# Two blocks of a language model on one core: rounded x at one address relation to the weights, with new segments and a smaller descriptor ring

## The chip, the cores and the metric

One core of one Trainium2 chip runs the whole program. The metric is the device time of one execution in microseconds; of repeated runs the median counts.

## The reference

Two transformer blocks in sequence on 512 tokens of width 1024, all in float32. The first norms x, projects it by `w_in`, and joins three branches (gated linear attention, a gated short convolution, attention in a window of 128) by sigmoid gates; the second puts 16 meta tokens ahead (528 rows), projects by `w_in_2`, and has an HGRN2 branch of 8 heads beside a Mamba-2 branch. Each ends in an FFN with a depthwise convolution of 3 taps. Cut to what is touched:

```python
def first_block(x, ...):
    u = rmsnorm(h, g_mix[l])
    z = u @ w_in[l]
    ...
    h = h + merged @ w_o[l]
    u = rmsnorm(h, g_ffn[l])
    hid = causal_dwconv(u @ w_up[l], ffn_conv_w[l])
    h = h + (jax.nn.silu(hid[..., :D_FF]) * hid[..., D_FF:]) @ w_down[l]
    return rmsnorm(h, g_final)

def second_block(x, meta_tokens, ...):
    h = jnp.concatenate([meta, x], axis=1)
    u = rmsnorm_2(h, norm1_w[l])
    proj = u @ w_in[l]
    ...
    h = h + jnp.concatenate([out_a, out_b], axis=-1) @ w_out[l]
    h = h + conv_glu_ffn(rmsnorm_2(h, norm2_w[l]), ...)
    return rmsnorm_2(h, final_norm_w)[:, N_META:, :]
```

## The kernel before, in words

Everything is feature-major: channels on the 128 partitions, tokens along the free dimension. The residual stream is `H`, 8 row groups (k) of 528 floats. A float32 product is made of three matmuls on rounded operands (float32r): `split` (L190) makes the high part on ACT and the remainder on DVE, for x into `XH` and `XL`; `WStream` does the same for the weights, `wh` and `wl`. The rms factor is not in x: it is multiplied in when a product is evacuated, so projections start before the norm's sums are done.

`WStream` (L53) loads all weights in the order in which the program takes them, in chunks of 8 tiles of 128 x 128 (1024 floats a partition, a load of 512 KB from SP's queue). `prep_to` casts a chunk to `wh` on ACT (L83) and subtracts for `wl` on DVE (L84); `take` asks for that two chunks ahead. `wraw` has two buffers, `wh` and `wl` three each, allocated in one row after the constants.

`gemm` (L234) runs over k and calls `pass3` (L228): for each k the matmuls of `wh` with `XH`, `wh` with `XL`, `wl` with `XH`, each over every segment, with the weights as the stationary operand and x as the moving one. A segment is a stretch of columns that fits a PSUM bank: block 1 has one of 512, block 2 two. After each k `tick` lets the lanes, generators with the work of the heads and scans, put a few small instructions in between; this and the order of the calls set the order on every queue, and the tile framework adds the waits. At the end of a product its evacuation runs on DVE and ACT.

Where x is used: block 1's `w_in` product with 512 columns (L528; the values product, L565, has x as the stationary operand), the gates, and the first FFN's up projection (`ffn`, L686); block 2's `w_in_2` product with `segs` of 264 + 264 for what needs the meta tokens and `segq` of 256 + 258 for what needs only the last 514 columns; the second FFN's up projection with 256 + 258. `FH`/`FL` hold the hidden layer of an FFN for its down projection, `MH`/`ML` the merged branches, `BH`/`BL` the branch outputs, `YH`/`YL` block 2's mixer output. Several pools start with a tile of 512 bytes (`pad1`, `pad2`, `pad3`) between a high part and its remainder.

The lines that place x:

```python
self.H = c.tile([P, KD, L], F32, name="H")
self.XH = c.tile([P, KD, L], F32R, name="XH")
self.XL = c.tile([P, KD, L], F32R, name="XL")
self.par_t = c.tile([P, NPAR], F32, name="par_t")
cm = c.tile([P, 3 * P + 24], F32, name="cm")
```

L is 528 and P is 128; `par_t` and `cm` take 2048 and 1632 bytes of a partition, `wraw` two times 4096, and then the `wh` buffers follow. Block 1 uses columns 8 to 520 of a row (`X1 = 8`), block 2 all 528.

Block 2's Mamba-2 branch loads tables from DRAM by POOL's queue (`m2_core`, L851: `seg` and `ei` for each chunk of 128 tokens); POOL's descriptors lie in a ring in SBUF ahead of the first tile, 16 KB of each partition by default.

Of the kernel before, what the change touches and what calls it, by code (L numbers as in the profile page):

```python
# [9 lines left out]
F32 = mybir.dt.float32  # L10
F32R = mybir.dt.float32r
# [7 lines left out]
P = 128  # L19
D = 1024  # L20
T = 512
META = 16
L = T + META
PADL = T + 32
X1 = 8
KD = D // P
NFF = 22
EPS = 1e-6
# [99 lines left out]
class Builder:  # L128
# [177 lines left out]
    def setup(self):  # L306
        nc, c = self.nc, self.const
        self.H = c.tile([P, KD, L], F32, name="H")
        self.XH = c.tile([P, KD, L], F32R, name="XH")
        self.XL = c.tile([P, KD, L], F32R, name="XL")  # L310
        self.par_t = c.tile([P, NPAR], F32, name="par_t")
        cm = c.tile([P, 3 * P + 24], F32, name="cm")
        self.four = cm[:, 3 * P:3 * P + 16]
        self.ident, self.le, self.ones = (cm[:, i * P:(i + 1) * P] for i in range(3))
        nc.scalar.preload_act_table_set("exp_and_others")
        nc.sync.dma_start(out=self.H[:, 0, META:L], in_=self.ins["xT"][:, 0])
        nc.scalar.dma_start(out=self.par_t[:, 0:8], in_=self.ins["par"][:, 0:8])
        self.W.load_to(0)
        for k in range(1, KD):
            nc.sync.dma_start(out=self.H[:, k, META:L], in_=self.ins["xT"][:, k])  # L320
            if k == 2:
                self.W.load_to(1)
        nc.gpsimd.dma_start(out=self.par_t[:, 8:NPAR], in_=self.ins["par"][:, 8:NPAR])
        nc.gpsimd.dma_start(out=cm[:, 0:3 * P + 16], in_=self.ins["cm"])
        nc.gpsimd.dma_start(out=self.H[:, :, 0:META], in_=self.ins["metaT"])

    def X(self, c0=META):
        return lambda k: (self.XH[:, k, :], self.XL[:, k, :])

    def sumsq(self, acc, k, src):  # L330
        if k == 0:
# [169 lines left out]

    def block1(self):
        nc, tc = self.nc, self.tc
        H, XH, XL = self.H, self.XH, self.XL
        self.W.prep_to(0)
        sums = [self.sq_acc(), self.sq_acc()]

# [9 lines left out]
            self.act(t, h, AF.Square)  # L517
            eng.tensor_tensor(out=sums[k % 2], in0=sums[k % 2], in1=t, op=ALU.add)
        for k in range(KD):
            self.split(XH[:, k, X1:X1 + T], XL[:, k, X1:X1 + T], H[:, k, META:L], self.par("g_mix", k))  # L520
            if k > 2:
                square(k - 3)
        for k in range(KD - 3, KD):
# [1 line left out]
        Rt = self.stat.tile([P, 4], F32, tag="Rt", name="Rt", bufs=1)  # L525
        R = self.r_tile()
        Rx = R[:, META:L]
        segs = [(X1, T)]  # L528
        X = self.X()
        WI = lambda c: [("w_in", k, c) for k in range(KD)]  # L530

        with ExitStack() as s1:
# [10 lines left out]
            with ExitStack() as s2:  # L543
# [14 lines left out]
                with tc.tile_pool(reuse_waits="tile", name="sp", bufs=1) as sp:  # L558
                    self.dist = sp.tile([P, 256], F32, name="dist")
                    nc.gpsimd.dma_start(out=self.dist, in_=self.ins["dist"])  # L560
                    sk = sp.tile([P, T], F32, name="sk")
                    svt = sp.tile([P, 4, P], F32, name="svt")
                    sq = [sp.tile([P, T], F32, name=f"sq{t}") for t in range(4)]
                    accs = [self.acc() for _ in range(4)]
                    for k in range(KD):  # L565
                        wh, wl = self.W.take([("w_in", k, GV + m * P) for m in range(4)])
                        for b in range(4):
                            c = slice(X1 + b * P, X1 + (b + 1) * P)
                            for i, (x, w) in enumerate(((XH, wh), (XL, wh), (XH, wl))):
                                self.mm(accs[b], x[:, k, c], w, start=k == 0 and i == 0, stop=k == 7 and i == 2)  # L570
                        if k == 5:
                            self.norm(self.token_rstd(sums, D, R, META, Rt), 4)
                        self.tick(4)

                    def ev_gv(a):
                        for b in range(4):
                            self.act(self.GVt[:, b, :], a[b], AF.Copy, scale=Rt[:, b:b + 1])
                    self.pend.append((ev_gv, accs))
                    self.flush(2)
                    self.lanes[1].add(self.meta_norm(), 6)  # L580
                    self.gemm16(wga, self.par("g_mix", 0, KD), [(META, T)], 3,
                                lambda a: self.mul(self.GAt[0:96], a[0][0:96], Rx[0:96]))
                    self.gemm(WI(SK), X, segs, lambda a: self.mul(sk, a[0], Rx))
                    sv = sp.tile([P, T], F32, tag="pT", name="sv", bufs=2)

                    def sv_gen():
                        ps = self.sm()
                        for n in range(4):
                            self.tr(ps[:, n * P:(n + 1) * P], sv[:, n * P:(n + 1) * P])
                        nc.scalar.copy(svt.rearrange("p a b -> p (a b)"), ps)  # L590
                        yield 1
                    self.gemm(WI(SV), X, segs, lambda a: self.mul(sv, a[0], Rx))
                    self.lanes[0].add(sv_gen(), 3)
                    for t in range(4):
                        self.gemm(WI(("sq", t)), X, segs,
                                  lambda a, t=t: self.stt(sq[t], a[0], 0.125, Rx, ALU.mult, ALU.mult))
                    self.flush(0, 1)
                    self.lanes[0].add(self.swa(sp, sq, sk, svt), 3)
                    sgr = [br.tile([P, T], F32, tag=f"blg{i}", name=f"sgr{i}") for i in range(4)]
                    for h in range(4):  # L600
                        def ev_gr(a):
                            t = gp.tile([P, T], F32, tag="a1", name="gr", bufs=1)
                            self.mul(sgr[h], a[0], Rx)
                            self.act(t, sgr[h], AF.Sigmoid)
                            self.mul(sgr[h], sgr[h], t)
                        self.gemm(WI(GR + h * P), X, segs, ev_gr)
                    glas = []
                    for h in range(4):
                        q = gp.tile([P, T], F32, tag="q", name="q", bufs=2)
                        kk = gp.tile([P, T], F32, tag="kk", name="kk", bufs=2)  # L610
                        self.gemm(WI(GQ + h * P), X, segs,
                                  lambda a: self.stt(q, a[0], float(P) ** -0.5, Rx, ALU.mult, ALU.mult))
                        self.gemm(WI(GK + h * P), X, segs, lambda a: self.mul(kk, a[0], Rx))
                        self.lanes[2].add(self.gla_head(gp, h, q, kk, sgr[h]), 2)
                    self.flush(0, 1)
# [48 lines left out]
            for m in range(KD):  # L664
                def ev_o(a, m=m):
                    h = H[:, m, META:L]
                    self.add(h, h, a[0])
                    self.split(XH[:, m, X1:X1 + T], XL[:, m, X1:X1 + T], h, self.par("g_ffn", m))
                    self.sumsq(sqa, m, h)
                self.gemm([("w_o", k, m * P) for k in range(KD)], lambda k: (MH[:, k, :], ML[:, k, :]), [(0, T)], ev_o)  # L670
        R = self.r_tile()
# [3 lines left out]
        nc.gpsimd.tensor_tensor(out=g1, in0=self.par("g_final", 0, 8), in1=self.par("norm1", 0, 8), op=ALU.mult)  # L675

        def after(m, h, _):
            self.split(XH[:, m, META:L], XL[:, m, META:L], h, g1[:, m:m + 1])
            self.split(XH[:, m, 0:META], XL[:, m, 0:META], H[:, m, 0:META], self.par("norm1", m))
            self.sumsq(sqh, m, h)  # L680
            self.ts(h, h, self.par("g_final", m), ALU.mult)
            self.sumsq(sqg, m, h)
# [3 lines left out]
    def ffn(self, up, cw, cb, down, R, after, zero):  # L686
        nc, tc, H = self.nc, self.tc, self.H
        W = T + 2
        segs = [(X1, T)] if zero else [(META - 2, 256), (META + 254, 258)]
        rsegs = [(META, T)] if zero else segs  # L690
        Xb = (self.XH, self.XL)
        with tc.tile_pool(reuse_waits="tile", name="fp", bufs=1) as fp:
            FH = fp.tile([P, NFF, T], F32R, name="FH")
            fp.tile([P, P], F32, name="pad3")
# [1 line left out]
            for j in range(NFF):  # L696
                cs = []
                for i in range(2):
# [6 lines left out]
                    def ev(a, i=i, f=f, u=u, c=c, cs=cs, j=j):  # L705
# [13 lines left out]
                        else:  # L719
                            self.mul(c, cs[0], c)  # L720
                            self.split(FH[:, j, :], FL[:, j, :], c)
                    self.gemm([(up, k, f * P) for k in range(KD)],
                              lambda k: (Xb[0][:, k, :], Xb[1][:, k, :]), segs, ev)
                    cs.append(c)
            for m in range(KD):
                def ev_d(a):
# [338 lines left out]

    def block2(self, sqh, sqg):
        nc, tc, st = self.nc, self.tc, self.stat
        H, XH, XL = self.H, self.XH, self.XL
        W2 = T + 2
        R = self.r_tile()  # L1070

# [20 lines left out]
                self.mul(H[:, k, META:L], H[:, k, META:L], R1[:, META:L])  # L1092
                yield 6
        self.norm(norm2(), 10)
        segs = [(0, 264), (264, 264)]
        segq = [(META - 2, 256), (META + 254, 258)]
        X = self.X()
        WI = lambda c: [("w_in_2", k, c) for k in range(KD)]

        with ExitStack() as sy:  # L1100
# [173 lines left out]
            with tc.tile_pool(reuse_waits="tile", name="hp", bufs=1) as hp:  # L1274
# [55 lines left out]
                def ev_o(m):  # L1330
                    def ev(a):
                        h = H[:, m, META - 2:L]
                        for ps, (c0, n) in zip(a, [(0, 256), (256, 258)]):
                            self.add(h[:, c0:c0 + n], h[:, c0:c0 + n], ps[:, 0:n])
                        self.split(XH[:, m, META - 2:L], XL[:, m, META - 2:L], h, self.par("norm2", m))
                        self.sumsq_w(sqa, m, h, W2)
                    return ev
                def y_k(i):
# [168 lines left out]
```

## Time and profile before

| | |
|---|---|
| median of 3 runs | 1769.63 us (1768.66 to 1769.98) |
| the profiled execution | 1771.67 us, of which span 1769.8 us |
| granted clock of TensorE, mean | 0.997 |
| busy: PE, PEld, DVE, ACT, POOL | 1738.0, 1534.6, 1089.8, 729.7, 123.9 us |
| read from HBM, written | 156.93 MB, 2.18 MB |

PE is TensorE's matmuls, PEld its loads of stationary operands, which run beside matmuls. A matmul is shown from its start to the modelled end of its pipeline, so consecutive ones overlap, and the spacing of starts is what a stream of them costs. The profile's clock is a share of 2.4 GHz. Block 1 runs to about 868 us: the values product and the branches to about 250, gates and branch products to about 455, `w_o` to about 500, the FFN's up projection to about 745 and its down projection to 868. Block 2 has the mixer to 1285, the output projection to 1365, the up projection to 1631 and the down projection after it.

### The profile page before, as it was taken

To read this page: it belongs to the slowest core of one execution; us is meant where nothing else is said; L and a number is where in the kernel's file an instruction comes from. 1 tells how busy PE (TensorE), PEld (TensorE's weight loads), DVE (VectorE), ACT (ScalarE), POOL (GpSimd) and SP (SyncE) were. 2 spreads that over 40 slices of the span, in tenths; PEclk is the share of its full clock that TensorE was granted. 3 is DMA by queue.
4 is the path that set the end of the run, shared out by engine and by line. 5 is a ranking of instruction groups with operands and counts; after the bars stand their busy time and mean duration, and the time that the engine had idled before them with its cause. 6 is when DMAs were issued, how large, how long until landed. Compare 5 with 4: busy or idle time off the path is not lost. (4 is left out here: it accounts for less than half of the span.)

```text
span 1769.8 us, 26970 instructions
## 1 busy us (share of the span) xinstructions
PE 1738.0 (98%) x11014; PEld 1534.6 (87%) x11014; DVE 1089.8 (62%) x1923; ACT 729.7 (41%) x1175; POOL 123.9 (7%) x203
## 2 busy tenths in 40 slices
PE   8999999999999999999998999999999999999997
PEld 6777778888888888888897999999999999999885
DVE  4476774444457777734488789767643667766332
ACT  4355443222344444433356545545432444444221
POOL 2000000000110000001112221000001000000000
PEclk9999999999999999999999999999999999999999
DMA  5222223332333333233333322122223223332331
GB/s 184 84 72 60 64 80 96 96 96 95 96 95 94 93 94 95 92 100 101 88 101 126 113 86 72 61 73 72 72 84 96 84 96 95 86 95 96 96 89 67
DMA packets 45691, 160.84 MB, mean 91 GB/s; under 512 B 5472, under 2 KB 5616, under 8 KB 45568
## 3 DMA queue, kind: packets, MB, share of 16 engines
q1 hardware_dynamic: 42480, 149.83, 27.3%
q0 software_dynamic: 2800, 9.03, 1.6%
q8 instruction: 86, 1.41, 0.3%
q14 instruction: 37, 0.30, 0.1%
q10 hardware_dynamic: 288, 0.27, 0.0%
HBM read 156.93 MB, written 2.18 MB: 90 GB/s over the span
## 5 line engine op out<-in xcount | busy, mean ns | idle before, releaser
L181 PE MATMUL acc<-XH,wh 128*128 128x512 f32 (+3 forms) x2320 | 633.2, 326 | 0.1
L181 PE MATMUL acc<-XL,wh 128*128 128x512 f32 (+3 forms) x2320 | 621.1, 321 | 0.0
L181 PE MATMUL acc<-XH,wl 128*128 128x512 f32 (+3 forms) x2320 | 619.0, 320 | 0.0
L83 ACT CAST wh<-wraw 128x1024 fp32r<-128x1024 f32 (+1 forms) x279 | 292.0, 1047 | 507.8 <-PE acc L181 441.8
L84 DVE TENSOR_TENSOR wl<-wraw,wh 128x1024 fp32r<-128x1024 f32 (+1 forms) x279 | 342.6, 1228 | 218.8 <-ACT wh L83 211.4
L181 PEld LDWEIGHTS acc<-XH,wh 128*128 128x128 f32 x2320 | 385.1, 189 | 45.2 <-issue 9.8
L181 PEld LDWEIGHTS acc<-XH,wl 128*128 128x128 f32 x2320 | 385.3, 189 | 33.8 <-issue 0.5
L181 PEld LDWEIGHTS acc<-XL,wh 128*128 128x128 f32 x2320 | 385.9, 189 | 32.9 <-issue 0.5
L181 PE MATMUL acc<-FH,wh 128*128 128x512 f32 x352 | 137.8, 392 | 0.0
L181 PE MATMUL acc<-FH,wl 128*128 128x512 f32 x352 | 137.1, 390 | 0.0
L181 PE MATMUL acc<-FL,wh 128*128 128x512 f32 x352 | 137.0, 389 | 0.0
L164 DVE SCALAR_TENSOR_TENSOR c<-u,par_t,c 128x512 f32<-128x512 f32 x176 | 131.8, 749 | 6.7 <-ACT c L178 3.7
L152 DVE TENSOR_TENSOR u<-acc,R 128x512 f32<-128x512 f32 (+2 forms) x132 | 63.8, 510 | 87.9 <-PE acc L181 84.7
L336 POOL TENSOR_TENSOR sqa<-sqa,sqt 128x512 f32<-128x512 f32 x27 | 40.8, 1513 | 735.5 <-ACT sqt L178 735.5
L181 PEld LDWEIGHTS acc<-FH,wl 128*128 128x128 f32 x352 | 66.1, 188 | 14.0
L181 PEld LDWEIGHTS acc<-FL,wh 128*128 128x128 f32 x352 | 66.1, 188 | 13.5
L181 PEld LDWEIGHTS acc<-FH,wh 128*128 128x128 f32 x352 | 66.1, 188 | 13.4
L178 ACT ACTIVATE FH<-c 128x512 fp32r<-128x512 f32 x44 | 27.8, 632 | 116.0 <-DVE c L152 116.0
L178 ACT ACTIVATE c<-u,par_t 128x512 f32<-128x512 f32 x88 | 67.6, 768 | 2.4 <-DVE u L152 2.2
L152 DVE TENSOR_TENSOR H<-H,acc 128x512 f32<-128x512 f32 (+2 forms) x41 | 22.6, 569 | 74.6 <-PE acc L181 74.6
L178 ACT ACTIVATE c<-c 128x512 f32<-128x512 f32 x44 | 27.8, 632 | 83.5 <-DVE c L164 83.5
L181 PE MATMUL acc<-yh,wh 128*128 128x256 f32 (+1 forms) x256 | 51.4, 282 | 0.1
(393 smaller groups left out, 1967.1 us busy)
## 6 DMA issues: line engine op xcount, KB each, us to landing
wraw<-in_wts SPq DMA_DIRECT2D x277, 512.0 KB, 3.6
seg<-cumd POOLq DMA_DIRECT2D x10, 512.0 KB, 4.3
H<-in_xT SPq DMA_DIRECT2D x8, 256.0 KB, 9.6
ei<-eid POOLq DMA_DIRECT2D x16, 128.0 KB, 3.3
out<-H SPq DMA_DIRECT2D x7, 256.0 KB, 2.7
wraw<-in_wts SPq DMA_DIRECT2D x2, 256.0 KB, 4.6
r<-in_r POOLq DMA_DIRECT2D x1, 272.0 KB, 3.2
r<-in_r POOLq DMA_DIRECT2D x1, 256.0 KB, 8.3
```

The costliest lines, as they stand in the source:

```text
L83: self.nc.scalar.copy(h[:, e], t[:, e])
L84: self.nc.vector.tensor_tensor(out=l[:, e], in0=t[:, e], in1=h[:, e].bitcast(F32), op=ALU.subtract)
L152: self.nc.vector.tensor_tensor(out=out, in0=a, in1=b, op=op)
L164: self.nc.vector.scalar_tensor_tensor(out=out, in0=a, scalar=s, in1=b, op0=op0, op1=op1)
L178: self.nc.scalar.activation(out=out, in_=a, func=func, scale=scale, **kw)
L181: self.nc.tensor.matmul(out, lhsT, rhs, start=start, stop=stop)
L336: self.nc.gpsimd.tensor_tensor(out=acc, in0=acc, in1=t, op=ALU.add)
```

## The change

The tiles of rounded x become flat: 8 x 640 floats each, with 512 bytes (`padx`) between the two, and two views of them. `X1` is block 1's and the first FFN's, rows of 512 floats one behind the other; `X2` is block 2's and the second FFN's, 528 columns of rows of 640 floats. Both begin 24 floats (96 bytes) into the tile. Segments are counted from the view's first column; in block 2 264 + 264 becomes 256 + 272, and the second FFN's x is written from column 0 of the row instead of 14. The three edits together take 7680 bytes more of each partition, and the ring of POOL's descriptors is cut from 16 KB to 8 KB.

```diff
@@ -22,7 +22,8 @@
...
 PADL = T + 32
-X1 = 8
+X0 = 24
+XW = 640
 KD = D // P
...
@@ -306,8 +307,13 @@
...
         self.H = c.tile([P, KD, L], F32, name="H")
-        self.XH = c.tile([P, KD, L], F32R, name="XH")
-        self.XL = c.tile([P, KD, L], F32R, name="XL")
+        self.X1, self.X2 = [], []
+        for n in ("XH", "XL"):
+            x = c.tile([P, KD * XW], F32R, name=n)
+            self.X1.append(x[:, X0:X0 + KD * T].rearrange("p (k t) -> p k t", t=T))
+            self.X2.append(x.rearrange("p (k t) -> p k t", t=XW)[:, :, X0:X0 + L])
+            if n == "XH":
+                c.tile([P, P], F32, name="padx")
         self.par_t = c.tile([P, NPAR], F32, name="par_t")
...
@@ -324,8 +330,8 @@
...
 
-    def X(self, c0=META):
-        return lambda k: (self.XH[:, k, :], self.XL[:, k, :])
+    def X(self, x):
+        return lambda k: (x[0][:, k, :], x[1][:, k, :])
 
...
@@ -501,7 +507,7 @@
...
         nc, tc = self.nc, self.tc
-        H, XH, XL = self.H, self.XH, self.XL
+        H, (XH, XL), (XH2, XL2) = self.H, self.X1, self.X2
         self.W.prep_to(0)
...
@@ -517,7 +523,7 @@
...
         for k in range(KD):
-            self.split(XH[:, k, X1:X1 + T], XL[:, k, X1:X1 + T], H[:, k, META:L], self.par("g_mix", k))
+            self.split(XH[:, k, :], XL[:, k, :], H[:, k, META:L], self.par("g_mix", k))
             if k > 2:
...
@@ -525,8 +531,8 @@
...
         Rx = R[:, META:L]
-        segs = [(X1, T)]
-        X = self.X()
+        segs = [(0, T)]
+        X = self.X(self.X1)
         WI = lambda c: [("w_in", k, c) for k in range(KD)]
...
@@ -565,7 +571,7 @@
...
                         for b in range(4):
-                            c = slice(X1 + b * P, X1 + (b + 1) * P)
+                            c = slice(b * P, (b + 1) * P)
                             for i, (x, w) in enumerate(((XH, wh), (XL, wh), (XH, wl))):
...
@@ -665,7 +671,7 @@
...
                     self.add(h, h, a[0])
-                    self.split(XH[:, m, X1:X1 + T], XL[:, m, X1:X1 + T], h, self.par("g_ffn", m))
+                    self.split(XH[:, m, :], XL[:, m, :], h, self.par("g_ffn", m))
                     self.sumsq(sqa, m, h)
...
@@ -675,8 +681,8 @@
...
         def after(m, h, _):
-            self.split(XH[:, m, META:L], XL[:, m, META:L], h, g1[:, m:m + 1])
-            self.split(XH[:, m, 0:META], XL[:, m, 0:META], H[:, m, 0:META], self.par("norm1", m))
+            self.split(XH2[:, m, META:L], XL2[:, m, META:L], h, g1[:, m:m + 1])
+            self.split(XH2[:, m, 0:META], XL2[:, m, 0:META], H[:, m, 0:META], self.par("norm1", m))
             self.sumsq(sqh, m, h)
...
@@ -686,9 +692,9 @@
...
         W = T + 2
-        segs = [(X1, T)] if zero else [(META - 2, 256), (META + 254, 258)]
-        rsegs = [(META, T)] if zero else segs
-        Xb = (self.XH, self.XL)
+        segs = [(0, T)] if zero else [(0, 256), (256, 258)]
+        rsegs = [(META, T)] if zero else [(META - 2, 256), (META + 254, 258)]
+        X = self.X(self.X1 if zero else self.X2)
         with tc.tile_pool(reuse_waits="tile", name="fp", bufs=1) as fp:
...
@@ -720,7 +726,7 @@
...
                     self.gemm([(up, k, f * P) for k in range(KD)],
-                              lambda k: (Xb[0][:, k, :], Xb[1][:, k, :]), segs, ev)
+                              X, segs, ev)
                     cs.append(c)
...
@@ -1065,7 +1071,7 @@
...
         nc, tc, st = self.nc, self.tc, self.stat
-        H, XH, XL = self.H, self.XH, self.XL
+        H, (XH, XL) = self.H, self.X2
         W2 = T + 2
...
@@ -1092,9 +1098,9 @@
...
         self.norm(norm2(), 10)
-        segs = [(0, 264), (264, 264)]
+        segs = [(0, 256), (256, 272)]
         segq = [(META - 2, 256), (META + 254, 258)]
-        X = self.X()
+        X = self.X(self.X2)
         WI = lambda c: [("w_in_2", k, c) for k in range(KD)]
...
@@ -1332,7 +1338,7 @@
...
                             self.add(h[:, c0:c0 + n], h[:, c0:c0 + n], ps[:, 0:n])
-                        self.split(XH[:, m, META - 2:L], XL[:, m, META - 2:L], h, self.par("norm2", m))
+                        self.split(XH[:, m, 0:W2], XL[:, m, 0:W2], h, self.par("norm2", m))
                         self.sumsq_w(sqa, m, h, W2)
...
@@ -1495,7 +1501,7 @@
...
 
-    nc = _bacc.Bacc("TRN2", target_bir_lowering=False, num_devices=1)
+    nc = _bacc.Bacc("TRN2", target_bir_lowering=False, num_devices=1, dynamic_dma_scratch_size=8192)
     ins = {n: nc.dram_tensor(f"in_{n}", s, F32, kind="ExternalInput").ap() for n, s in IN_SHAPES.items()}
...
```

## Rows read from the trace of the kernel before

**Rows 1.** The page: busy time by engine, granted clock in 40 slices.

```profile
PE 1738.0 (98%) x11014; PEld 1534.6 (87%) x11014; DVE 1089.8 (62%) x1923; ACT 729.7 (41%) x1175; POOL 123.9 (7%) x203
...
PEclk9999999999999999999999999999999999999999
```

**Rows 2.** Waits of PE, the two longest (us in total, times, longest).

```profile
PE sm L184 <- DVE xf L164: 6.4, 3, 2.8
PE acc L181 <- ACT XH L178: 5.8, 1, 5.8
```

**Rows 3.** Groups of matmuls by shape, 512 columns (count, busy us, mean ns).

```profile
L181 PE MATMUL acc<-XH,wh 128*128 128x512 f32 x784 | 312.5, 399 | 0.0
...
L181 PE MATMUL acc<-XH,wl 128*128 128x512 f32 x784 | 309.3, 394 | 0.0
...
L181 PE MATMUL acc<-FH,wh 128*128 128x512 f32 x352 | 137.8, 392 | 0.0
...
L181 PE MATMUL acc<-MH,wh 128*128 128x512 f32 x64 | 24.9, 389 | 0.0
...
L181 PE MATMUL acc<-bh_gla,wh 128*128 128x512 f32 x32 | 12.6, 394 | 0.0
...
L181 PE MATMUL acc<-bh_conv,wh 128*128 128x512 f32 x32 | 12.4, 389 | 0.0
```

**Rows 4.** PE by window: length, busy (matmuls), clock, DMA share, GB/s.

```profile
520.00:720.00 200.00, 200.00 (x865) 1.00 0.32 98
760.00:860.00 100.00, 100.00 (x442) 1.00 0.30 95
1390.00:1610.00 220.00, 220.00 (x1844) 1.00 0.29 92
1310.00:1360.00 50.00, 50.00 (x422) 1.00 0.33 96
```

**Rows 5.** Timeline of PE, 303 to 313 us (start, duration, instruction).

```profile
304.72 0.39 PE L181 MATMUL acc<-bh_conv,wh 128*128 128x512 f32 x1
...
308.80 0.39 PE L181 MATMUL acc<-XH,wh 128*128 128x512 f32 x1
...
309.50 0.39 PE L181 MATMUL acc<-XH,wh 128*128 128x512 f32 x1
...
310.19 0.40 PE L181 MATMUL acc<-XH,wh 128*128 128x512 f32 x1
...
311.59 0.39 PE L181 MATMUL acc<-XH,wh 128*128 128x512 f32 x1
```

**Rows 6.** Preparation of a weight chunk on ACT and DVE, and its load.

```profile
L83 ACT CAST wh<-wraw 128x1024 fp32r<-128x1024 f32 x277 | 290.8, 1050 | 505.9 <-PE acc L181 441.8 <-issue 59.6 <-DMA wraw<-in_wts 2.8
...
L84 DVE TENSOR_TENSOR wl<-wraw,wh 128x1024 fp32r<-128x1024 f32 x277 | 341.2, 1232 | 212.0 <-ACT wh L83 204.6 <-PE sm L181 4.3
...
wraw<-in_wts SPq DMA_DIRECT2D x277, 512.0 KB, 3.6
```

**Rows 7.** Both FFNs' up projections by window: PE, PEld, DVE, ACT, POOL.

```profile
500.00:745.00 245.00, 245.00 (x1068) 198.82 (x1067) 173.53 (x228) 106.07 (x136) 6.44 (x46) 1.00 0.30 95
...
1365.00:1631.00 266.00, 266.00 (x2228) 265.81 (x2227) 182.33 (x289) 110.47 (x140) 3.69 (x2) 1.00 0.29 92
```

**Rows 8.** Groups by shape in block 2: a matmul of 264 columns, evacuations.

```profile
L181 PE MATMUL acc<-XH,wh 128*128 128x264 f32 x448 | 96.1, 295 | 0.1
...
L152 DVE TENSOR_TENSOR u<-acc,R 128x256 f32<-128x256 f32 x44 | 18.7, 425 | 43.5 <-PE acc L181 43.5
...
L152 DVE TENSOR_TENSOR mu<-acc,R 128x264 f32<-128x264 f32 x24 | 9.4, 425 | 1.7 <-PE acc L181 1.6
```

**Rows 9.** POOL's burst (timeline), `seg` loads, ACT's wait for them.

```profile
921.62 1.12 POOL L864 DMA_DIRECT2D seg<-cumd  x2 [0.61 <-DMA cumd<-ct]
...
seg<-cumd POOLq DMA_DIRECT2D x10, 512.0 KB, 4.3
...
L178 ACT ACTIVATE seg<-seg,dv 128x128 f32<-128x128 f32 x64 | 20.5, 390 | 16.8 <-DMA seg<-cumd 14.5 <-PE acc L181 2.1
```

## The prediction

> **What bounds the kernel now.** I read the page from the top. TensorE is busy for 98% of the span at a granted clock of 1.00 (the 2.4 GHz level) from the first slice to nearly the last, and DVE, the next engine, for 62% [rows 1]. The list of PE's waits is short: the largest two, 6.4 us for `xf` in block 2 and 5.8 us for `XH` at the start, are most of it [rows 2]. The chain that ended last covers 3% of the span and says nothing on the middle. So the kernel is as long as its stream of matmuls, and the question is how far apart their starts are.
>
> Next the groups of matmuls by shape, because a change of addresses can only show where equal shapes take different times. They do: a matmul of 512 columns has a mean of 389 ns when its moving operand is `MH` or `bh_conv`, 392 for `FH`, and 394 to 399 for `XH` and `XL` [rows 3]. A duration holds the pipeline's depth, so the spacing of starts is read from counts. In the up projection of the first FFN (moving `XH`, `XL`) 865 matmuls lie in 200 us, 231.2 to 231.8 ns each, depending on how the two at the edges count; in its down projection (moving `FH`, `FL`) 442 lie in 100 us, 226.2 to 227.3 ns [rows 4]. One stage shows both back to back: the `conv` and `swa` products from 304.72 to 308.80 us are 18 steps, 226.7 ns each, and the gate product that follows takes 12 steps to 311.59 us, 232.5 ns each [rows 5]. Same shape, engines and clock, so the operands' place is the suspect.
>
> The tile sizes give that place. A weight tile of a chunk is 512 bytes wide, so all weights start at one remainder modulo 512. `FH`, `FL`, `MH`, `ML` and the `bh`/`bl` tiles have rows of 2048 bytes and, with the pads, start at that remainder: relation 0 on every k. Rows of `XH` are 2112 bytes, so the relation moves by 64 from k to k and is 0 only once in eight, at k = 1. After the change it comes to 0 for every k of block 1: from row 0 of `XH` to the first weight tile there are 20480 + 512 + 20480 + 2048 + 1632 + 8192 - 96 = 53248 bytes, 104 times 512. Net, memory moves by 7680 - 8192 = -512 bytes, so every later pool keeps its relation.
>
> **The change, part by part.**
>
> *Block 1, moving x.* 784 k-steps of three matmuls (`wh` with `XH`, `wh` with `XL`, `wl` with `XH`), 2352 in all [rows 3]. I take 226.7 ns, the pace of `conv`/`swa`, in place of 231.7. In the gates (192 steps) and the first FFN's up projection (352) nothing interrupts the stream: 1632 x 5.0 ns = 8.2 us. The other 240 steps run before 250 us, with the small matmuls of gla and attention between them. After a break the pace doesn't come back at once: the gla products, also at relation 0 but just behind a gate product at another one, have a mean of 394 ns, and `conv` behind them has 389 [rows 3]. I take 4 of the 5 ns: 720 x 4 = 2.9 us. The gla products gain the same entry: 96 x about 4 ns = 0.4 us. Sum -11.5 us; bounds -12.2 (all at 5 ns) and -4.2 (rival 2).
>
> *Cover for a faster stream.* A chunk of weights feeds 24 matmuls: 5.56 us before, 5.44 after. It needs 1.05 us of ACT, 1.23 us of DVE and 3.6 us from issue to landing [rows 6], and the down projection already lives on it at 5.44. In the up projection DVE is busy 173.5 of 245 us [rows 7], 72% of 241. Nothing new becomes late.
>
> *Block 2, segments 264 + 264 to 256 + 272.* the page's 448 x 3 halves [rows 8], the same columns. The relation to the weights now takes another multiple of 32 on each k and half; it becomes 0 for both halves on every k. No row shows short matmuls settled at relation 0, so I bound it. The second FFN's up projection (256 + 258) has 1844 matmuls in 220 us, 119.3 ns each, and the output projection with `yh`, `yl`, whose relation differs by row, 422 in 50 us, 118.5 [rows 4]: two mixtures of relations, nearly one pace. PEld is busy there for 265.8 of 266 us against 198.8 of 245 in block 1 [rows 7]: the loads of weights fill the time, and the moving operand has little to give. Low bound: 119.3 to 118.5 on 4608 short matmuls (1344 of 264, 2112 of the second FFN, 1152 of 256 + 258 elsewhere, whose relation becomes 56 and not 0), -3.7 us. High bound: 226.7 ns at 512 columns is 13.3 ns over 512 columns at 2.4 GHz; the same surplus on 257 columns is 120.4, +1.1 x 4608 = +5.1 us. I take 0, as the rows of the second FFN are nearest and PEld is full there. A part of 272 columns isn't hidden worse than 264 by more than the columns it takes from its neighbour.
>
> *Evacuations.* A half of 264 costs DVE 425 ns, one of 256 as much [rows 8]: the same work. The writes of x (`split`) are as many, in other places. Writing `XH2` over `XH` while rows of 512 are still wanted would be a new wait, but the up projection's last read lies 66 matmuls ahead of the first such write: 0.
>
> *First product (`GV`).* There x is the stationary operand, in 96 matmuls, behind 5.8 us of waiting for `XH` [rows 2]. Alignment may give 0.5 us; the load of x sets that stage, I take 0.
>
> *Descriptor ring of 8 KB.* POOL's densest burst begins at 921.62 us with two `seg` loads issued in 1.12 us, one right behind the other [rows 9]; nothing there shows a full ring, and I take 0. If each of the ten `seg` loads had to wait out one landing of 4.3 us, 43 us of POOL time would go, in a stage where ACT already waits 14.5 us for `seg` [rows 9].
>
> **Sum**: -11.5 + 0 = -11.5 us. The profiled execution took 1771.67 us (span 1769.8), 2.0 over the median of the runs shown; so 1760.2 there and 1758.1 for the median.
>
> **The rivals.**
>
> 1. *Place is not the cause.* Then the up projection is slower for its evacuations (one each 24 matmuls instead of 66), and nothing changes: 1769.6, give or take 1. Against it: gates and `conv` products in one stage, 226.7 and 232.5 [rows 5], with evacuations behind each. The Trainium skill, "TensorE: Matmul & The Clock Gate", section "Step-by-step: what each phase is for", speaks for this rival: it gives PE two independent SBUF read ports and says that loading the next weights takes no bandwidth from the running matmul. By that rule the change is worth 0; the rows differ by 5 ns, so I follow the rows. Chance 0.04.
>
> 2. *Relation 0 is not enough.* The one k of eight that has it now, at 309.50 us, takes 0.69 us to 310.19, against 0.70 for the step before it [rows 5], not 0.68. If x in block 1 stays at 690 ns a step, 784 x 5.3 = 4.2 us come back: 1765.4. For it: gla is at relation 0 and slow too. Against: gla's twelve matmuls run into the 389 of `conv`; `MH` and `FH` hold 389 to 392 over hundreds [rows 3]. Chance 0.07.
>
> 3. *Block 2 gains too*, by what the `yh` pace allows on all 4608 short matmuls or twice that: -3.7 to -7.4 us more, 1750.7 to 1754.4. Chance 0.12.
>
> 4. *Block 2 loses: slower than before.* With x and weights in step, a matmul of 256 columns is about as long as the load beside it, and the two could meet on every column instead of drifting past each other. The dearest surplus in the trace is that of `XH` at 512 columns, 231.7 - 213.3 = 18.4 ns; on 257 columns 125.5 instead of 119.3, +6.2 x 4608 = +28.6 us, net 1786.7. It decides from 2.5 ns a short matmul (11.5 / 4608). Against: 256 + 258 columns at mixed relations nowhere show such a spread. Chance 0.05.
>
> **How the numbers follow.** Forecast 0.72 at 1758.1, its own range 1753 to 1763 (block 2's bounds around -11.5, with a little for the share of block 1 that doesn't settle). For 8 in 10 the range goes from 1752 to 1764: it leaves out rivals 1 and 4 (0.09), most of rival 2 and the far end of rival 3. About 0.2% (3.5 us) is what this measurement can tell from no change. Faster by more: forecast, rival 3 and most of rival 2, 0.89; within: rival 1 and the rest of rival 2, 0.06; slower: 0.05.
>
> **What the profile after will show.** Right: `XH`/`XL` of 512 columns at 389 to 390 ns, in the first FFN's up projection some 882 matmuls in 200 us, gla at 389; PE still at 98%. Wrong in step one: `XH` at 394 or more, or 870 in 200 us (rival 2). Block 2: the second FFN within 1 ns of 119.3 a matmul; at 121 or more rival 4 is on its way. The ring: POOL waits between the issues at the `seg` burst. A gain in the matmuls that a longer list of PE waits eats would prove the cover wrong.

## The result and the profile after

The changed kernel takes 1759.38 us in the median of four runs (1758.69 to 1760.91), the kernel before 1769.61 on the same chip: ratio 0.9944, interval 0.9927 to 0.9961, so 10 us less, give or take 3. Its profiled execution took 1758.69 us (span 1756.9); against the 1771.67 of the one before that is 13 us, more than the medians differ, because the first was 2.1 us over its median and the second 0.7 under.

The page after (answers to [rows 1]):

```profile
PE 1725.6 (98%) x11014; PEld 1533.3 (87%) x11014; DVE 1090.0 (62%) x1923; ACT 729.4 (42%) x1175; POOL 125.1 (7%) x203
...
PEclk9999999999999999999999999999999999999998
```

PE is as full as it was, at the same clock: its stream got shorter. The groups by shape (answers to [rows 3, 8]):

```profile
L182 PE MATMUL acc<-XH,wh 128*128 128x512 f32 x784 | 310.1, 396 | 0.0
L182 PE MATMUL acc<-XH,wl 128*128 128x512 f32 x784 | 306.4, 391 | 0.0
...
L182 PE MATMUL acc<-FH,wh 128*128 128x512 f32 x352 | 137.7, 391 | 0.0
...
L182 PE MATMUL acc<-bh_gla,wh 128*128 128x512 f32 x32 | 12.4, 389 | 0.0
...
L182 PE MATMUL acc<-bh_conv,wh 128*128 128x512 f32 x32 | 12.4, 389 | 0.0
```

`XH` at 512 columns went from 399 to 396 ns for the first matmul of a k-step and from 394 to 391 for the third; gla went from 394 to 389, and what had 389 kept it. The means of `XH` hold the matmuls before 250 us, which have waits and small matmuls between them. From 500 to 735 us, in the first FFN's up projection alone, they had 393 to 395 before:

```profile
L181 PE MATMUL acc<-XL,wh 128*128 128x512 f32 x333 | 131.7, 395 | 0.0
L181 PE MATMUL acc<-XH,wl 128*128 128x512 f32 x333 | 130.9, 393 | 0.0
```

In the changed kernel:

```profile
L182 PE MATMUL acc<-XH,wh 128*128 128x512 f32 x344 | 134.0, 390 | 0.0
L182 PE MATMUL acc<-XL,wh 128*128 128x512 f32 x343 | 133.4, 389 | 0.0
L182 PE MATMUL acc<-XH,wl 128*128 128x512 f32 x343 | 133.4, 389 | 0.0
```

The windows show the stream itself (answers to [rows 4]; the windows of the down projection and the output projection lie 10 us earlier):

```profile
520.00:720.00 200.00, 200.00 (x884) 1.00 0.32 97
750.00:850.00 100.00, 100.00 (x443) 1.00 0.31 95
1390.00:1610.00 220.00, 220.00 (x1835) 1.00 0.30 92
1300.00:1350.00 50.00, 50.00 (x422) 1.00 0.31 95
```

884 matmuls where 865 were, as close together as in the down projection. In the second FFN 1835 where 1844 were: a little slower. The timeline of a gate product, gla, `conv` and `swa` (answers to [rows 5]):

```profile
296.20 0.39 PE L182 MATMUL acc<-XH,wh 128*128 128x512 f32 x1
...
296.88 0.39 PE L182 MATMUL acc<-bh_gla,wh 128*128 128x512 f32 x1
...
299.60 0.39 PE L182 MATMUL acc<-bh_conv,wh 128*128 128x512 f32 x1
...
302.32 0.39 PE L182 MATMUL acc<-bh_swa,wh 128*128 128x512 f32 x1
```

From 296.20 to 302.32 us are 27 matmuls across four operands, 226.7 ns each without a change of pace; before, the gate product had 232.5 and gla ran unsettled. The waits of PE are the same two (answers to [rows 2]), and ACT's wait for `seg` is 14.6 us, as before (answers to [rows 9]):

```profile
PE acc L182 <- ACT XH L179: 5.8, 1, 5.8
PE sm L185 <- DVE xf L165: 4.9, 3, 2.0
```

```profile
L179 ACT ACTIVATE seg<-seg,dv 128x128 f32<-128x128 f32 x64 | 20.5, 390 | 17.4 <-DMA seg<-cumd 14.6 <-PE acc L182 2.8
```

From the starts of the matmuls, I summed the k-steps (three matmuls, six with two segments) of each stage, each from its first matmul to that of the next step:

| stage, moving x | steps | before, us | after, us |
|---|---|---|---|
| `w_in` before the gates | 241 | 220.5 | 218.8 |
| gates | 191 | 133.4 | 130.7 |
| first FFN, up | 352 | 246.5 | 241.4 |
| second FFN, up | 352 | 254.8 | 255.9 |
| mixer of block 2, its first matmul to that of the output projection | | 413.8 | 410.9 |

Block 1 gives 9.5 us, and gla's 32 steps 0.4 more; the second FFN takes 1.1 back. The mixer's 2.9 us are not put down to the change, for a reason that the runs below give. Where a k-step's length is given in ns below, it is the mean over the undisturbed steps of that stage: those whose matmuls, and the first of the next step, follow each other with nothing between and no wait.

### The profile page after: what moved, and what is told of

The parts are those of the page before. It is cut to its first block, busy times and chain, and to the rows that moved or that the text cites. A ratio compares the mean times of both kernels' runs of the same rounds, so it can differ in the third digit from the quotient of the medians.

```text
span 1756.9 us, 26969 instructions
## 1 busy us (share of the span) xinstructions
PE 1725.6 (98%) x11014; PEld 1533.3 (87%) x11014; DVE 1090.0 (62%) x1923; ACT 729.4 (42%) x1175; POOL 125.1 (7%) x203
```

## The experiments

**Which part pays.** The first kernel has block 1's part alone, in the old tiles, without 640-column rows, small ring or new segments:

```diff
+        flat = lambda x: x.rearrange("p k l -> p (k l)")[:, X0:X0 + KD * T].rearrange("p (k t) -> p k t", t=T)
+        self.X1 = (flat(self.XH), flat(self.XL))
```

> Block 1's rows of 512 columns at relation 0, laid into the old tiles; block 2's layout, its segments of 264 + 264 and the ring of 16 KB as before. Theory 'relation in block 1': the matmuls of 512 columns with XH and XL in the gates and the first FFN's up projection fall to 389 to 390 ns, gla to 389, the groups of block 2 stay; the time falls by 9 to 11.5 us, to 1758 to 1761. Rival 'block 2 or the move of memory carries a good part': the same groups fall, but the time stays above 1764.

1758.39 us, ratio 0.9933 (0.9916 to 0.9949). Its groups by shape:

```profile
L181 PE MATMUL acc<-XH,wh 128*128 128x512 f32 x784 | 309.9, 395 | 0.0
L181 PE MATMUL acc<-XH,wl 128*128 128x512 f32 x784 | 306.4, 391 | 0.0
...
L181 PE MATMUL acc<-XH,wh 128*128 128x264 f32 x448 | 96.1, 295 | 0.1
...
L181 PE MATMUL acc<-bh_gla,wh 128*128 128x512 f32 x32 | 12.4, 389 | 0.0
```

Block 1 as in the changed kernel (389 to 390 ns from 500 to 735 us here too), block 2 as before, and the whole gain is there, for no memory. The counterpart keeps everything but block 1's view:

```diff
-            self.X1.append(x[:, X0:X0 + KD * T].rearrange("p (k t) -> p k t", t=T))
+            self.X1.append(x[:, 0:KD * L].rearrange("p (k t) -> p k t", t=L)[:, :, 8:8 + T])
```

> Block 2's rows of 640, segments of 256 + 272 and the small ring as in the changed kernel; block 1 reads rows of 528 columns again, at the relations of before. Theory 'relation in block 1': XH and XL of 512 columns are back at 394 to 399 ns, the second FFN's up projection at about 1836 matmuls in 220 us, and the time is within 2.5 us of before, 1767 to 1771. Rival 'block 2 carries a good part': below 1766.

1769.46 us, ratio 0.9999 (0.9990 to 1.0009):

```profile
520.00:720.00 200.00, 200.00 (x865) 1.00 0.31 96
1390.00:1610.00 220.00, 220.00 (x1836) 1.00 0.30 92
```

865 again in the first FFN and 1836 in the second. Block 2's rows, segments and the ring are worth nothing that the time shows. The mixer took 413.1 us here with the very block 2 of the changed kernel, which had 410.9, and 412.8 in the next run with that of before, which had 413.8: one execution's mixer wanders by a few us, and 2.9 us of it prove nothing.

The ring alone:

```diff
-    nc = _bacc.Bacc("TRN2", target_bir_lowering=False, num_devices=1)
+    nc = _bacc.Bacc("TRN2", target_bir_lowering=False, num_devices=1, dynamic_dma_scratch_size=8192)
```

> The kernel before with the ring of descriptors at 8 KB and nothing else: all tiles move down by 8192 bytes together. Theory 'relation': no group changes, 1769.6 give or take 1.5. Rival 'ring': POOL's DMA issues get longer or wait, the waits of ACT for seg grow beyond 14.5 us, and the time rises by more than 3 us; rival 'absolute addresses': the time falls by more than 3 us.

1770.16 us, ratio 1.0001 (0.9992 to 1.0011). Groups of PE, the burst of POOL and ACT's wait:

```profile
L181 PE MATMUL acc<-XL,wh 128*128 128x512 f32 x784 | 310.4, 396 | 0.0
```

```profile
920.72 1.12 POOL L864 DMA_DIRECT2D seg<-cumd  x2 [0.60 <-DMA cumd<-ct]
921.83 2.47 POOL L869 DMA_DIRECT2D ei<-eid  x4
```

```profile
L178 ACT ACTIVATE seg<-seg,dv 128x128 f32<-128x128 f32 x64 | 20.5, 390 | 18.9 <-DMA seg<-cumd 18.9
```

The issues are as long as in [rows 9] and follow each other as closely. ACT waits 18.9 us instead of 14.5 for `seg`, more than expected, but the changed kernel with the same ring has 14.6, and the time doesn't move. All tiles lie 8192 bytes lower here, and a move of everything by that much doesn't count. As 8192 is a multiple of 256, this says nothing on smaller moves.

**What the relation does.** The next kernels give each stage a view of x with its own start in the same tiles, so that the relation is constant over k but chosen. In floats (4 bytes), `XH` and `XL`, 24 being relation 0:

```diff
+WIN, UP, WIN2, UP2 = (56, 56), (40, 40), (56, 56), (30, 30)
...
+            for v, o in ((self.X1, WIN[i]), (self.XU, UP[i])):
+                v.append(x[:, o:o + KD * T].rearrange("p (k t) -> p k t", t=T))
+            for v, o, w in ((self.X2, WIN2[i], L), (self.XU2, UP2[i], T + 2)):
+                v.append(x.rearrange("p (k t) -> p k t", t=XW)[:, :, o:o + w])
```

> The changed kernel with each stage's view of x begun elsewhere in the same tiles, so that the relation to the weights is constant over k but not 0: 128 bytes for block 1's w_in product, 64 for the first FFN's up projection, 128 for block 2's w_in_2 product (184 for the halves of 256 + 258), 24 for the second FFN's up projection. Theory 'a multiple of 256 is what counts': block 1's matmuls of 512 columns go back to 232 to 233 ns from start to start (697 a k-step) in both stages, and the time to 1767 to 1770. Theory 'a constant relation is enough, whatever its size': they stay at 226.7 (680 a step), time 1758 to 1761. Second FFN: the rows of before at relation 24 took 715 ns a step of six, so 715 against 720 now, 1.8 us less in that stage.

1778.27 us in one execution, slower than before. Windows in the gates, the first and the second FFN's up projection:

```profile
300.00:400.00 100.00, 100.00 (x434) 1.00 0.32 95
520.00:720.00 200.00, 200.00 (x876) 1.00 0.32 97
1390.00:1610.00 220.00, 220.00 (x1799) 1.00 0.28 89
```

The first window holds the branch products too, so I give the gates' steps from the starts. A constant relation isn't enough, and that theory falls. Of the other, 128 costs what was said (699.4 ns a step in the gates), but 64 costs 686.7 instead of 697, and 24 in the second FFN 735 where I had read 715 from steps of before at that relation. Those steps stood in a row of changing relations; a step's time is not its own. Part of the 1778 us lies in block 2: its `w_in_2` steps took 739.1 ns at 128 against 732.2 at 0 in the changed kernel, and its mixer 417.6 us, the longest of all profiles.

```diff
+WIN, UP, WIN2, UP2 = (88, 88), (8, 8), (8, 8), (8, 8)
```

> The changed kernel with constant relations of 256 bytes for block 1's w_in product and of -64 bytes for the three other stages (first FFN's up projection, w_in_2, second FFN's up projection). Theory 'the relation counts modulo 256': 256 is as good as 0, so the gates stay at 680 ns a k-step; at -64 the first FFN goes to 690 to 700 ns a step and the second to 720 to 735. Rival 'only 0 is good, and the distance counts': the gates rise to 690 or more. Time 1765 to 1775 by the first, 1768 to 1778 by the second.

1765.30 us:

```profile
300.00:400.00 100.00, 100.00 (x443) 1.00 0.32 95
520.00:720.00 200.00, 200.00 (x859) 1.00 0.32 93
1390.00:1610.00 220.00, 220.00 (x1871) 1.00 0.32 94
```

256 is as good as 0 (443 in the gates' window, 680.2 ns a step). At -64 the first FFN has 700.0 ns, as expected, but the second 706.7, the shortest steps of 256 + 258 so far and well under the range I gave.

```diff
+WIN, UP, WIN2, UP2 = (24, 32), (24, 40), (40, 40), (72, 72)
```

> The changed kernel with XH at relation 0 in block 1 and only XL moved, by 32 bytes for the w_in product and by 64 for the first FFN; in block 2 both at 64 for w_in_2 and at 192 for the second FFN. Theory 'every matmul pays for its own relation': in block 1 only one matmul of three moves, so a step costs 682 to 686 ns (a third of the 7 to 19 ns that relations of 64 and 128 cost); 192 in the second FFN costs what -64 costs there. Theory 'a break in the pattern spoils the steps behind it too': 687 or more.

1764.29 us. Moving `XL` alone costs 695.0 ns a step in the gates (by 32) and 696.0 in the first FFN (by 64), more than moving both by 64 (686.7): the theory that each matmul pays for its own relation falls, and its rival holds. All three spacings of a step grew in the gates, to 231.5, 233.0 and 230.7 ns from 226.7, though two of the three matmuls read `XH` at relation 0. 192 gives 706.7, as -64 does: 256 is the period for short matmuls too.

The kernel without the 512 bytes between `XH` and `XL`:

```diff
-            if n == "XH":
-                c.tile([P, P], F32, name="padx")
```

> The changed kernel without the 512 bytes between XH and XL, so that both stand at one place modulo 2048 and all relations to the weights stay 0. Theory 'the relation to the weights is all': no group changes, 680 ns a step in block 1, 720 in the second FFN, time 1758 to 1761. Rival 'the two parts of x need different places': steps of 685 ns or more in block 1, time above 1763.

1761.06 us in one execution, at the edge of the range, with steps of 680.1 in the first FFN and 720.0 in the second: the pad does nothing. And the segments:

```diff
-        segs = [(0, 256), (256, 272)]
+        segs = [(0, 264), (264, 264)]
```

> The changed kernel with halves of 264 + 264 in the rows of 640 (the second half's relation is then 32), and with XL moved by 32 bytes in the second FFN. Theory 'short matmuls hardly mind, the split is free': the w_in_2 steps stay within 3 ns of 732 and the second FFN within 3 ns of 720. Rival 'aligned halves are worth it': 738 or more for 264 + 264. Rival 'a shifted XL is better, as the rows of yh and yl (710 on average) suggest': 712 or less in the second FFN, 2.8 us less there.

1757.89 us. The undisturbed steps of `w_in_2` take 720.6 ns with 264 + 264 in rows of 640, against 732.2 with 256 + 272, so both expectations on them miss. The 11.6 ns are not the split's alone: the second half's relation went from 0 to 32 with it, and 256 + 272 took 721.0 ns in the kernel that had this stage at -64, 731.5 in the one that had it at 64. The gain doesn't reach the time: the stage's 222 steps sum to 219.9 us against 220.3, as what the clean steps save is waited for in those with small matmuls between. `XL` moved by 32 gives 716.7 in the second FFN, neither 720 nor 712.

**A version that beats both kernels.** Relation 0 in block 1, 264 + 264, -64 in the second FFN, rows of 576, no pad, small ring:

```diff
+WIN, UP, WIN2, UP2 = (24, 24), (24, 24), (24, 24), (8, 8)
-XW = 640
+XW = 576
```

> Relation 0 in block 1, halves of 264 + 264 at relation 0 in w_in_2, relation -64 in the second FFN's up projection; rows of 576 columns, which are a multiple of 256 bytes too, no pad, ring of 8 KB. If the relations act stage by stage, as measured: 680 ns a step in block 1, 720.6 in w_in_2, 706.7 in the second FFN; against the changed kernel 13.3 ns x 352 = 4.7 us less in the second FFN and nothing that shows from w_in_2, so 1753.5 to 1756, 14 to 16 us under before. Rival: rows of 576 are at relation 0 modulo 256 but not 512, and that counts: block 2's steps 5 ns or more above these.

1755.02 us, ratio 0.9922 (0.9909 to 0.9936), 14.4 us under before:

```profile
300.00:400.00 100.00, 100.00 (x443) 1.00 0.32 95
520.00:720.00 200.00, 200.00 (x885) 1.00 0.31 96
1390.00:1610.00 220.00, 220.00 (x1871) 1.00 0.30 94
```

The stages add up as measured apart (680.1, 720.7, 706.7 ns), and rows of 576 columns, 2304 bytes, serve as well: 256 is the period that counts.

**The neighbours.** Two more of these in block 2, and one in both blocks:

```diff
+WIN, UP, WIN2, UP2 = (24, 24), (24, 24), (8, 8), (16, 16)
...
+WIN, UP, WIN2, UP2 = (24, 24), (24, 24), (0, 0), (0, 0)
...
+WIN, UP, WIN2, UP2 = (16, 16), (32, 32), (24, 24), (12, 12)
```

> The changed kernel with halves of 264 + 264 at relation -64 in w_in_2 and with relation -32 in the second FFN. Interpolated between -64 (706.7 ns a step) and 0 (720.0): the second FFN at 710 to 716. The clean steps of w_in_2 at or below 721; the mixer's length as before, within 2 us, whatever they do, if that stage is set by its chains and not by the stream.

> The changed kernel with halves of 264 + 264 at relation -96 in w_in_2 and with relation -96 in the second FFN. If -64 is an optimum, the second FFN lies above 706.7 ns a step; if the steps get shorter the further the halves lie ahead of the weights, below 703. The mixer's length as before, within 2 us.

> The fastest version with relation -32 for block 1's w_in product, +32 for the first FFN and -48 for the second FFN. If 0 is the optimum for 512 columns, the gates and the first FFN's up projection rise above 680 ns a step (half of the 6.7 that +64 costs would be 683; half of the 20 that -64 costs 690). Rival 'the optimum lies beside 0': one of them falls below 680. The second FFN between -64 (706.7) and -32 (710.1).

1757.07, 1761.79 and 1772.64 us. The last kernel's windows:

```profile
300.00:400.00 100.00, 100.00 (x434) 1.00 0.31 95
520.00:720.00 200.00, 200.00 (x859) 1.00 0.32 95
1390.00:1610.00 220.00, 220.00 (x1835) 1.00 0.30 92
```

-32 in the second FFN gives 710.1, -96 gives 720.0; in `w_in_2` the clean steps have 721.5 and 721.4, just over the 721 expected. The mixer took 413.0 and 414.3 us in these two, within 2 us of the kernel before (413.8) but not of the changed kernel (410.9), which by its wander decides nothing. The interpolations of the last run are wrong throughout: +32 and -32 cost 20 ns a step in block 1, not 3 to 10, and -48 gives 720.0, above both neighbours. 0 is the best of those tried for 512 columns, but no slope leads to it.

| relation, bytes | 512 columns, ns a step | 256 + 258 columns, ns a step |
|---|---|---|
| changing with k (before) | 695 | 716.8 |
| 0 | 680.1 | 720.0 |
| 24 | | 735.0 |
| 32 | 700.0 | |
| 64 | 686.7 | |
| 128 | 699.4 | |
| 192 or -64 | 700.0 (-64) | 706.7 |
| 256 | 680.2 | |
| -32 | 700.0 | 710.1 |
| -48 | | 720.0 |
| -96 | | 720.0 |

The figures are means over k. At one relation throughout, steps need not be equal: those at 24 in the second FFN take 734, 736, 742 and 728 ns for k = 0 to 3 and the same again for 4 to 7, while those at 0 all take 720.

**Whose start counts.** In the values product of block 1 the roles are swapped: weights move, and x is the stationary operand. Its matmuls in the changed kernel (first and last of 11), and in the one with x shifted by 128 bytes there:

```profile
27.76 0.39 PE L182 MATMUL acc<-wh,XL 128*128 128x512 f32 x1
...
30.03 0.39 PE L182 MATMUL acc<-wl,XH 128*128 128x512 f32 x1
```

```profile
27.67 0.39 PE L183 MATMUL acc<-wh,XL 128*128 128x512 f32 x1
...
29.98 0.40 PE L183 MATMUL acc<-wl,XH 128*128 128x512 f32 x1
```

That is 227 against 231 ns for each of ten spacings, with the moving operand, the weights, in the same place. The other kernels agree: over the second half of this product the median spacing is 227 ns with x at 0 or 256 there, 230 to 234 otherwise. So the start of x counts in either role, and a rival by which only the moving operand's own start matters is out. Another isn't: by the tile sizes the weights begin at one remainder modulo 256 in every kernel here, since all moves of memory are multiples of 256. Whether the difference of the two starts counts, as the word relation says, or the start of x by itself, no run tells.

## Why the prediction was right, and where not

The forecast of 1758.1 us lies 1.3 under the measured median. That it is so close is in part luck: the steps above account for 8.8 us of gain (9.5 + 0.4 - 1.1) where 11.5 were forecast, and the medians differ by 10.2, give or take 3. Point by point:

- *Moving x in block 1*, the term that carried it: right in cause and nearly in size. The gates and the first FFN gave 7.8 us for 8.2, gla the 0.4. The step that was mis-sized is "I take 4 of the 5 ns" for the 720 matmuls before 250 us: their sum fell by 1.7 us, 2.4 ns each. Steps that nothing interrupts fell there from 696.0 to 683.1 ns, but 74 of the 241 are longer, 44 of them for small matmuls between, and their sum did not fall (104.3 us before, 104.7 after). The sign set for this term, `XH` at 389 to 390 ns, shows in the gates and the first FFN; over the whole kernel `XH` has 396 and 391, for the same reason.
- *Cover*: held. PE's waits did not grow, and the up projection keeps 884 matmuls in 200 us with the same chunks to prepare.
- *Block 2*: 0 was taken, and the kernel with block 2's part alone shows 0. But the reason given, that the loads of weights fill the time and "the moving operand has little to give", is the step that fell: with x at 24 the second FFN's up projection takes 261.2 us, at -64 251.3, at 0 255.9. The rows of before hid this because they mix four relations, modulo 256, in eight k; their evenness was a mean, no floor. The change put these steps at a relation 3.2 ns worse than the mixture, 1.1 us in that stage.
- *Split, ring, evacuations*: nothing of the ring shows. At the relation of the change, 256 + 272 takes 732.2 ns a step and 264 + 264 takes 720.6, but 256 + 272 at -64 takes 721.0, so the 272 columns are not what is worse; the time doesn't show the difference.
- *"Relation 0" modulo 512*: narrower than need be; 256 is the period for both lengths. So "the one k of eight that has it now" should be two, and the trace of the kernel before shows it: in its first FFN's up projection k = 1 and k = 5 both take 690.0 ns a step, and k = 0 to 3 (695.3, 690.0, 699.8, 696.9) come again as k = 4 to 7 (695.1, 690.0, 700.0, 697.2). The 5.3 ns in rival 2 should be 5.1 (695.1 less 690), which moves its time by 0.2 us.

Rival 1 (place is no cause) is out: one shape in one stage runs at 226.7, 228.9 or 233.3 ns by the start of x alone. The Trainium skill, "TensorE: Matmul & The Clock Gate", section "Step-by-step: what each phase is for", has the two reads of PE independent of each other, from which rival 1 took 0; the runs have up to 20 ns a step of three matmuls by the start of x, and the measurement decides. Rival 2 (no settling) is out: 680 holds for whole stages. Rivals 3 and 4 named something real in block 2, a gain or a loss by relation, but not at relation 0; at -64 the gain, at 24 the loss.

What stays open is why: whether the reads of the two operands meet anywhere is not shown. The order of the relations (0, 64, 128, then 32, -32 and -64 for 512 columns; another order for 256) follows no distance, and the cost of moving `XL` alone shows that a matmul's neighbours count. No run here looks inside.

## What to carry to other kernels

Where matmuls of one shape have different spacings in one trace, compare the starts of their operands before blaming the stage: here 5 ns in 232 lay in the remainder of (moving minus stationary) modulo 256, changed by moving x alone. Make that remainder constant over the loop and then measure some values of it, for each length of the moving operand by itself, since the best one for 512 columns was not the best for 257, and a constant one can be worse than a changing one. Views of one tile are enough for it; the memory and the smaller ring of this change were not needed for its gain.

## What the runs showed of the hardware that I had not expected

- A relation of 24 bytes costs 15 ns a step of six short matmuls against 0, and -64 saves 13, though loads of weights fill the window from 1365 to 1631 us to the last 0.2 of 266 us [rows 7]. That window holds this stage, which begins at 1376 us, and the last 11 us of the output projection, which ends there and not at 1365.
- The cost by relation is uneven: for 512 columns +64 costs 6.6 ns a step and +32 costs 20, for 256 + 258 -48 is worse than -32 and -64.
- Steps at one relation inside a changing row don't have the time of that relation: 690 ns at 0 among others against 680 when all are at 0, 715 at 24 against 735.
